# A decoder layer's gated MLP: PSUM banks from a free list, a look-ahead of one chunk, additions and low halves one product later

## The chip, the cores and the metric

The kernel runs on one core of a Trainium2 chip. Its engines run side by side, each through its own queue in order: TensorE (PE, with PEld for the loading of weights), VectorE (DVE), ScalarE (ACT), GpSimd (POOL) and SyncE (SP, which here issues every DMA). They meet at semaphores. The metric is the device time of one execution in microseconds (us); lower is better. "Lnnn" is a line of the kernel before.

## What is computed

One layer: a mixing sub-layer (pooling and dilated attention), then a channel sub-layer, a gated MLP with a causal convolution of width 3. The change touches the second:

```python
def conv_ffn(h, w_up, conv_w, conv_b, w_down):
    S = h.shape[1]
    up = h @ w_up
    gate, val = up[..., :D_FF], up[..., D_FF:]
    gp = jnp.pad(gate, ((0, 0), (CONV_WIDTH - 1, 0), (0, 0)))
    gate = gp[:, 0:S] * conv_w[0] + gp[:, 1:S + 1] * conv_w[1] + gp[:, 2:S + 2] * conv_w[2] + conv_b
    return (jax.nn.gelu(gate, approximate=True) * val) @ w_down
```

SEQ and D_MODEL are 1024, D_FF is 2816, everything is float32. Every norm has an adaLN modulation; its gate for this sub-layer, a row of 1024 numbers, is worked out from `w_ada` during the MLP.

## The kernel before

**The up product.** D_FF is cut into 22 chunks of 128 channels. Per chunk the kernel needs four blocks, gate and value for two halves of the sequence, each 128x512, and gets them by Strassen's scheme with seven products instead of eight. A product is a sum over four blocks of 128 of the contraction, and each factor is split in a high and a low part of float32 (high·high, high·low, low·high), so that a product is 12 matmuls (L1042 to L1044) into one PSUM bank of 128x512. Products are written (n, c): n from 1 to 7, c the chunk. Products 1 and 2 make the gate of the first half of the sequence, 5, 6, 3, 7 and 4 the rest.

**What each product needs.** Its stationary side is a piece of `w_up` or a sum of pieces. `prep(n, c)` (L1119) issues the DMA or has POOL add the sums t1, t2, t3, t4 (L1117), has ACT round the high half (L119) and DVE subtract the low half (L171). It runs LEAD = 6 products ahead, and finished pieces lie in a ring of seven. `raw4` holds two chunks of raw weights (`load4`, 1024 KB each).

**What follows each product.** DVE adds it from PSUM into `UU` (u), `VV` (v) and `GG`: `evac` is issued straight after the product (n = 6: L1052 and L1053; 3: L1055; 7: L1057 and L1058; 4: L1063), and `first(c)` takes products 1 and 2 (an ACT copy, then DVE at L1021). After product 4 ACT multiplies `GG` by the last tap (L1064), DVE adds the two other taps (L1146, L1148), ACT applies GELU (L1150) and DVE multiplies with the value (L1153, `gated`). Every second chunk has four more DVE subtractions and additions (L1165, `act_sum`) for the down product. Results go to DRAM (`gscr`).

**The order.** PE, ACT, DVE and POOL run exactly in the order in which the code issues (`manual_schedule`). `steps` (L1168) lists the products: chunk by chunk 5, then the 4 of the chunk before, 6, two products of look-ahead (2 and 1 of a later chunk), 3, 7. Products 1 and 2 of chunks 0 to 3 are made before the loop (AHEAD = 3). In the chunks of `SKIP` = (0, 7, 14) and in the last chunk there is no look-ahead: such a chunk has five products instead of seven. With the last product, (4, 21), `steps` has 146.

**Banks.** PSUM has eight banks, and `SLOTS` gives chunk c the pair c mod 4. Look-ahead runs three chunks ahead and so holds three of the four pairs. Within a chunk, products 2, 5 and 3 write one bank of the pair, and 1, 6, 7 and 4 the other, one after another.

**The gate row.** `gate_acc` (L1183) loads eight blocks of `w_ada` (256 KB), each into the same buffer `gm`, and DVE adds each up (L1187, L1189), one block per product; this is done twice, once from 14 products before chunk 16 on and once from 14 before chunk 19 on. `gate_sum` sums over partitions with one matmul.

**Start and end.** The operands of the Strassen products (`sums` L926, `parts` L171) are made by DVE and ACT from the normed input at the turn from the mixing sub-layer; POOL does some of it (L970 four sums of weights, L926 once, L171 once). After the 146th product the down product starts on PE at once; its pieces are prepared ahead too (`prep_down`).

Of the kernel before, what the change touches and what calls it, by code (L numbers as in the profile page):

```python
# [88 lines left out]
SKIP = (0, 7, 14)  # L89
LAST_4 = 0  # L90
ENDS = 6
S_LAG = 3
# [8 lines left out]
def block_kernel(ctx: ExitStack, tc: tile.TileContext, x, pos, cols, rows, consts, w_ada_a, w_ada_b, w_in_u,  # L101
# [744 lines left out]
    if True:  # L846
# [73 lines left out]
        def sums(cols, which):  # L920
            m11, m12, m21, m22, m1 = (x[:, :, cols] for x in (a11, a12, a21, a22, SRC["s1"]))
            for i in which:
                eng, o, a, b, op = ((nc.vector, m1, m22, m21, ALU.subtract), (nc.vector, m11, m1, m11, ALU.add),
                                    (nc.vector, m12, m11, m12, ALU.subtract),
                                    (nc.vector if cols == lo_t else nc.gpsimd, m21, m11, m22, ALU.subtract))[i]
                eng.tensor_tensor(o, a, b, op)  # L926
# [9 lines left out]
        with tc.manual_schedule(engines={ET.PE, ET.Activation, ET.DVE, ET.Pool}):  # L936
# [22 lines left out]
            for c in range(AHEAD + 1):  # L959
                if c + 2 <= AHEAD:  # L960
                    up_load(c + 2)
                if c == 2:
                    raws = [rp.tile([P, 2, 512], F32, name="raws", tag="raw") for _ in range(2)]
                    raws = [t[:, i] for t in raws for i in range(2)]
                    for i in range(4):
                        nc.sync.dma_start(raws[i], w_up[0, :, i])
                    b11, b21, b12, b22 = raws
                    t2r = cp.tile([P, 512], F32, name="t2r", tag="macc")
                    for o, a, b in ((b11, b11, b12), (t2r, b11, b22), (b12, b12, b22), (b21, b21, t2r)):
                        nc.gpsimd.tensor_tensor(o, a, b, ALU.add)  # L970
                    p0 = r2.tile([P, 4, 512], F32R, name="p0", tag="r2b")
# [44 lines left out]
            def first(c):  # L1016
                if c >= NC_FF:
                    return
                a, b = (bank(x) for x in SLOTS[c % 4])
                copy(nc.scalar, UU[:, c % 2], a)  # L1020
                nc.vector.tensor_add(GG[:, c % 2, 0:512], UU[:, c % 2], b)  # L1021
# [6 lines left out]
            def new_piece():  # L1028
# [3 lines left out]
            USES = {1: ("11", 1, 0), 2: ("12", 2, 1), 3: ("s4", 3, 1), 4: ("22", "t4", 0), 5: ("s1", "t1", 1),  # L1032
                    6: ("s2", "t2", 0), 7: ("s3", "t3", 0)}

            def product(n, c):
                a, w, b = USES[n]
                wh, wl = W.pop((w, c))
                o = bank(LAST_4 if (n, c) == (4, NC_FF - 1) else SLOTS[c % 4][b])
                for k in range(4):
                    ks = slice(k * P, (k + 1) * P)  # L1040
                    ah, al = side(a, k)
                    nc.tensor.matmul(o, wh[:, ks], ah, start=k == 0, stop=False)  # L1042
                    nc.tensor.matmul(o, wh[:, ks], al, start=False, stop=False)  # L1043
                    nc.tensor.matmul(o, wl[:, ks], ah, start=False, stop=k == 3)  # L1044
# [3 lines left out]
            def evac(n, c):  # L1048
                a, b = (bank(x) for x in SLOTS[c % 4])
                u, v = UU[:, c % 2], VV[c % 3]  # L1050
                if n == 6:
                    nc.vector.tensor_sub(u, u, a)  # L1052
                    nc.vector.tensor_add(v[:, hi], u, b)  # L1053
                elif n == 3:
                    nc.vector.tensor_add(v[:, lo], v[:, hi], b)  # L1055
                elif n == 7:
                    nc.vector.tensor_add(u, u, a)  # L1057
                    nc.vector.tensor_add(v[:, hi], v[:, hi], a)  # L1058
                elif n == 4:
                    if c == NC_FF - 1:  # L1060
                        a = bank(LAST_4)
                    g = GG[:, c % 2]
                    nc.vector.tensor_add(g[:, hi], u, a)  # L1063
                    nc.scalar.activation(cv, g, AF.Identity, bias=cl("conv_b", c), scale=cl("conv_w2", c))  # L1064
                    LATER.append((0, lambda: taps(c, g)))
                    LATER.append((1, lambda: gated(c, v)))
            v, u = VV[0], UU[:, 0]
            a, b = (bank(x) for x in SLOTS[0])
# [12 lines left out]
            parts("s4", all_t)  # L1081
            nc.vector.tensor_sub(u, u, a)
            nc.vector.tensor_sub(v[:, hi], v[:, hi], a)
            product(3, 0)
            more = r1.tile(half, F32R, name="more", tag="rb2")
# [5 lines left out]
            product(7, 0)  # L1091
            evac(3, 0)
            first(1)
            A["22"] = [(0, *(r2.tile(half, F32R, name="b22", tag=t) for t in ("r2a", "r2b")))]
            parts("22", all_t, lo_eng=nc.gpsimd)
            more = r1.tile([P, 8, 512], F32R, name="more", tag="rb0")
            ring += [(more[:, 2 * i], more[:, 2 * i + 1]) for i in range(4)] + [(p1[:, 0], p1[:, 1])]
# [6 lines left out]
    with tc.manual_schedule(engines={ET.PE, ET.Activation, ET.DVE, ET.Pool}):  # L1104
# [4 lines left out]
        def fetch(src):  # L1109
            r, w = new_raw(), new_piece()  # L1110
            nc.sync.dma_start(r, src)
            split(r, *w)
            return w
# [5 lines left out]
        def prep(n, c):  # L1119
# [10 lines left out]
            elif n in (1, 2):  # L1130
                W[n, c] = fetch(w_up[c, :, n - 1])
                return
# [9 lines left out]
            W[key, c] = new_piece()  # L1142
            split(src, *W[key, c])
# [24 lines left out]
        steps, done, FIRST = [], AHEAD, {}  # L1168
        for c in range(NC_FF):
            one = []  # L1170
# [9 lines left out]
            FIRST[len(steps) - 3 + (len(ahead) == 0)] = c + 1  # L1180
# [12 lines left out]
        def gate_sum(hf, c):  # L1193
            o = bank(SLOTS[(c + 2) % 4][1])
# [3 lines left out]
            nc.vector.tensor_tensor(row, o[0:1], row, ALU.add)  # L1198
# [5 lines left out]
            LATER.append((2, fin))  # L1204

        EXTRA, LATER = {}, []
# [5 lines left out]
        for j in range(NC_FF // 2):  # L1212
            i4 = steps.index((4, 2 * j + 1))
            for i in range(4):
                EXTRA.setdefault(i4 + S_LAG + i, []).append(lambda j=j, i=i: act_sum(2 * j + 1, i))
# [33 lines left out]
        ready = [4]  # L1249

        def prep_up(to):
            while ready[0] < min(to, len(steps)):
                prep(*steps[ready[0]])
                ready[0] += 1

        prep_up(5)
        evac(7, 0)
        prep_up(6)
        for i, (n, c) in enumerate(steps):
            if i < 4:  # L1260
                continue
            for f in EXTRA.get(i, ()):
                f()
            prep_up(i + 1 + min(LEAD, i - 2))
# [18 lines left out]
        for d, f in LATER:  # L1283
            f()
        for i in sorted(EXTRA):
            if i >= len(steps):
                for f in EXTRA[i]:
                    f()

    with tc.manual_schedule(engines={ET.PE}):  # L1290
# [12 lines left out]
        def dbank(n, t):  # L1303
            return bank(((6, 7, 2, 3), (0, 1, 4, 5))[DOWN.index(n) % 2][t])
# [125 lines left out]
```

## Time and profile before

| | |
|---|---|
| median of 3 runs | 1137.0 us (1135.84 to 1140.2) |
| the profiled execution | 1138.1 us |
| its span, first to last instruction | 1136.3 us |
| PE busy | 1056.9 us (93%) |
| DVE busy | 862.7 us (76%) |
| ACT busy | 473.7 us (42%) |
| POOL busy | 239.5 us (21%) |
| mean granted clock of TensorE | 0.981 |

Matmuls overlap in the record (one of 128x512 is shown with 0.39 us, and the next starts 0.23 us after it), so PE's busy time says less than the distance from start to start. A row of the timeline has start, duration, engine, line, operation, output and inputs, and in brackets how long the engine had stood idle and what ended the wait. A row of the windows has the stretch, its length, the busy time of PE, PEld, DVE, ACT and POOL (with the number of instructions), the granted clock, the DMA share and GB/s.

### The profile page before, as it was taken

Reading aid. Unit: us, or ns where it says so; the run is one execution under the profiler, and the core shown is the slowest. Engines: PE = TensorE matmul, PEld = TensorE weight load, DVE = VectorE, ACT = ScalarE, POOL = GpSimd, SP = SyncE. Lnnn points to the kernel's source line nnn. Section 1 sums busy time; section 2 is a strip of 40 time slices with the busy share of each in tenths; the row PEclk is TensorE's granted clock in tenths of the full one; section 3 lists DMA queues with packets and bytes.
Section 4 is the critical chain, followed back from the end, with each engine's and each line's share of the span. In section 5 each row is a group of like instructions: output and inputs, shape, how many; then the busy total and the mean of one; then the engine's idle time right before and its main releaser. Section 6 shows DMA issues by size and latency. Waiting matters only on the chain.

```text
span 1136.3 us, 15489 instructions
## 1 busy us (share of the span) xinstructions
PE 1056.9 (93%) x5174; PEld 881.7 (78%) x5174; DVE 862.7 (76%) x1881; ACT 473.7 (42%) x958; POOL 239.5 (21%) x138
## 2 busy tenths in 40 slices
PE   5899999999999998889998999969979999999996
PEld 4799997889888876667777778757757888888885
DVE  8964457864657799778787887858768898856797
ACT  6564342433544686433332333322223355544542
POOL 0000000000000004433342333323233153302460
PEclk9999999999999999899999999989989999999999
DMA  9651446262211543133424332335434589666653
GB/s 351 214 165 38 136 115 187 70 192 60 82 46 39 201 151 130 47 112 130 149 78 154 112 123 109 121 112 175 143 109 139 178 289 351 193 200 216 211 187 111
DMA packets 85147, 168.32 MB, mean 148 GB/s; under 512 B 9158, under 2 KB 25926, under 8 KB 81356
## 3 DMA queue, kind: packets, MB, share of 16 engines
q1 hardware_dynamic: 85068, 167.35, 44.4%
q8 instruction: 40, 0.66, 0.2%
q14 instruction: 39, 0.32, 0.1%
HBM read 134.47 MB, written 32.84 MB: 147 GB/s over the span
## 4 chain that ended last, share of the span: by engine, by line
PE 56%; DVE 23%; DMA 8%; issue 7%; ACT 4%; POOL 1%; SPq 0%; DVEq 0%; ACTq 0%; POOLq 0%
PE PS L1311 6%; PE PS L1313 6%; PE PS L1312 6%; PE PS L1042 6%; PE PS L1044 5%; PE PS L1043 5%; PE PS L223 5%; PE PS L225 4%; PE PS L224 4%; DMA gm<-in_w_ada_b_dram 3%; DMA mraw<-in_w_ada_b_dram 2%; DVE cv L1148 2%; PE PS L686 2%; DVE more L171 2%; PE PS L656 2%
## 5 line engine op out<-in xcount | busy, mean ns | idle before, releaser
L223 PE MATMUL PS<-wh,hh 128*128 128x384 f32 x336 | 125.6, 374 | 0.0
L225 PE MATMUL PS<-wh,hl 128*128 128x384 f32 x336 | 114.3, 340 | 0.0
L224 PE MATMUL PS<-wl,hh 128*128 128x384 f32 x336 | 114.1, 340 | 0.0
L970 POOL TENSOR_TENSOR raws<-raws 128x512 f32<-128x512 f32 x2 | 4.0, 1993 | 438.9 <-DMA raws<-in_w_up_dram 438.9
L171 DVE TENSOR_TENSOR more<-raws,more 128x512 fp32r<-128x512 f32 x79 | 68.6, 876 | 27.4 <-ACT more L119 27.4
L119 ACT ACTIVATE more<-raws 128x512 fp32r<-128x512 f32 x79 | 48.8, 622 | 68.9 <-PE PS L1043 48.8
L1117 POOL TENSOR_TENSOR raws<-rw 128x512 f32<-128x512 f32 x28 | 50.9, 1818 | 94.4 <-DVE more L171 81.8
L223 PEld LDWEIGHTS PS<-wh,hh 128*128 128x128 f32 x336 | 64.1, 191 | 7.9 <-issue 4.8
L665 ACT ACTIVATE pm<-pm,nm 128x128 f32<-128x128 f32 (+1 forms) x96 | 42.4, 443 | 65.2 <-DVE nm L663 44.0
L1064 ACT ACTIVATE cv<-GG,col 128x1024 f32<-128x1024 f32 x22 | 27.4, 1244 | 98.5 <-DVE GG L1063 98.5
L224 PEld LDWEIGHTS PS<-wl,hh 128*128 128x128 f32 x336 | 64.2, 191 | 0.6 <-issue 0.5
L225 PEld LDWEIGHTS PS<-wh,hl 128*128 128x128 f32 x336 | 64.0, 190 | 0.0
L1150 ACT ACTIVATE cv<-cv 128x1024 f32<-128x1024 f32 x22 | 23.3, 1061 | 89.3 <-DVE cv L1148 89.3
L1042 PE MATMUL PS<-a,more 128*128 128x512 f32 x144 | 56.0, 389 | 0.0
L1043 PE MATMUL PS<-a,more 128*128 128x512 f32 x144 | 56.0, 389 | 0.0
L1044 PE MATMUL PS<-a,more 128*128 128x512 f32 x144 | 56.0, 389 | 0.0
L1042 PE MATMUL PS<-b,more 128*128 128x512 f32 x84 | 35.8, 427 | 20.8 <-DVE VV L1058 18.0
L659 DVE CUSTOM_DVE_ANT_0 pm<-PS,cst 128x128 f32<-128x128 f32 (+1 forms) x96 | 30.9, 348 | 30.0 <-PE PS L656 26.2
L1311 PE MATMUL PS<-tail 128*128 128x512 f32 x128 | 49.8, 389 | 0.0
L1312 PE MATMUL PS<-tail 128*128 128x512 f32 x128 | 49.8, 389 | 0.0
L1313 PE MATMUL PS<-tail 128*128 128x512 f32 x128 | 49.8, 389 | 0.0
L1148 DVE SCALAR_TENSOR_TENSOR cv<-GG,col,cv 128x1022 f32<-128x1022 f32 x22 | 47.6, 2165 | 0.7
(381 smaller groups left out, 3157.0 us busy)
## 6 DMA issues: line engine op xcount, KB each, us to landing
rw<-in_w_up_dram SPq DMA_DIRECT2D x21, 1024.0 KB
gscr<-VV SPq DMA_DIRECT2D x66, 256.0 KB
mraw<-in_w_ada_b_dram SPq DMA_DIRECT2D x48, 256.0 KB
R<-in_w_down_dram SPq DMA_DIRECT2D x48, 256.0 KB
raw<-in_w_in_u_dram SPq DMA_DIRECT2D x24, 384.0 KB
wa<-in_w_ada_a_dram SPq DMA_DIRECT2D x8, 1024.0 KB
raws<-in_w_up_dram SPq DMA_DIRECT2D x28, 256.0 KB
R<-gscr SPq DMA_DIRECT2D x27, 256.0 KB
```

Of the source, the lines that this page charges most:

```text
L171: (lo_eng or nc.vector).tensor_tensor(wl, raw, wh.bitcast(F32), ALU.subtract)
L223: nc.tensor.matmul(o, a, wh[:, c0:c0 + 384], start=k == 0, stop=False)
L224: nc.tensor.matmul(o, a, wl[:, c0:c0 + 384], start=False, stop=False)
L225: nc.tensor.matmul(o, b, wh[:, c0:c0 + 384], start=False, stop=k == 7)
L1042: nc.tensor.matmul(o, wh[:, ks], ah, start=k == 0, stop=False)
L1043: nc.tensor.matmul(o, wh[:, ks], al, start=False, stop=False)
L1044: nc.tensor.matmul(o, wl[:, ks], ah, start=False, stop=k == 3)
L1117: nc.gpsimd.tensor_tensor(t, a, b, ALU.add)
L1148: nc.vector.scalar_tensor_tensor(cv[:, 2:], g[:, :S - 2], cl("conv_w0", c), cv[:, 2:], op0=ALU.mult, op1=ALU.add)
L1311: nc.tensor.matmul(o, gh[:, ts_], wh, start=k == 0, stop=False)
L1312: nc.tensor.matmul(o, gh[:, ts_], wl, start=False, stop=False)
L1313: nc.tensor.matmul(o, gl[:, ts_], wh, start=False, stop=k == KD - 1)
```

## The change

Five things change in the up product. (1) A bank is no longer bound to a chunk: `idle` is a list of free banks, `product` takes the one that has been free longest, and `done_with` gives a bank back when the code issues its last read. (2) `SKIP` is (0, 1, 4), so that from chunk 5 on products 1 and 2 are made one chunk ahead and not three or fewer; chunks 7 and 14 have seven products, chunks 1 and 4 five. (3) `evac` and the subtraction of a low half are issued one product later (LAG_EV, LAG_LO); the high half on ACT keeps its place. (4) What was hung behind a product by lists of delays (`LATER`, `EXTRA`) is now a list of tasks by step. (5) At the start the four sums of weights (L970), one subtraction (L926) and the low half of operand 22 (L171, 128x2048) go from POOL to DVE, and 5 and 6 of chunk 0 are ordered anew.

```diff
-SKIP = (0, 7, 14)
-LAST_4 = 0
+SKIP = (0, 1, 4)
-S_LAG = 3
+LAG_LO, LAG_EV = 1, 1
...
-                    for o, a, b in ((b11, b11, b12), (t2r, b11, b22), (b12, b12, b22), (b21, b21, t2r)):
-                        nc.gpsimd.tensor_tensor(o, a, b, ALU.add)
...
+            used = {(n, c): SLOTS[c][n - 1] for c in range(AHEAD + 1) for n in (1, 2)}
+            idle = []
+
+            def done_with(n, c):
+                idle.append(used[n, c])
+                return bank(used.pop((n, c)))
 
             def product(n, c):
-                a, w, b = USES[n]
+                a, w = USES[n]
                 wh, wl = W.pop((w, c))
-                o = bank(LAST_4 if (n, c) == (4, NC_FF - 1) else SLOTS[c % 4][b])
+                used[n, c] = idle.pop(0)
+                o = bank(used[n, c])
...
                 if n == 6:
-                    nc.vector.tensor_sub(u, u, a)
-                    nc.vector.tensor_add(v[:, hi], u, b)
+                    nc.vector.tensor_sub(u, u, done_with(6, c))
+                    nc.vector.tensor_add(v[:, hi], u, done_with(5, c))
...
             sums(hi_t, (0, 1))
+            start_sum("t1", b11, b11, b12)
             start_piece("t1", b11)
             parts("s1", hi_t)
             first(0)
-            sums(hi_t, (2, 3))
+            product(5, 0)
+            sums(hi_t, (2,))
             parts("s2", hi_t)
+            start_sum("t2", t2r, b11, b22)
             start_piece("t2", t2r)
-            product(5, 0)
+            product(6, 0)
+            first(1)
             start_piece(3, b22)
-            product(6, 0)
-            nc.vector.tensor_add(v[:, hi], u, b)
             pairs_of("s4")
             parts("s4", all_t)
...
             product(3, 0)
+            sums(hi_t, (3,))
+            start_sum("t3", b12, b12, b22)
...
-            W[key, c] = new_piece()
-            split(src, *W[key, c])
+            w = W[key, c] = new_piece()
+            copy(nc.scalar, w[0], src)
+            return lambda: lower(src, *w)
...
+        def later_evac(n, c):
+            if n in (3, 4, 6, 7):
+                at_step(now[0] + LAG_EV, lambda: (evac(n, c), finish_4(c) if n == 4 else None))
...
+            to = i + 1 + min(LEAD, i - 2)
+            prep_up(to, to - LAG_LO)
...
-            due = [f for d, f in LATER if d == 0]
-            LATER[:] = [(d - 1, f) for d, f in LATER if d]
-            for f in due:
-                f()
+            run_tasks(i)
+            while not idle:
+                run_tasks(10**6, 1)
             product(n, c)
-            evac(n, c)
-            first(FIRST.get(i, NC_FF))
+            later_evac(n, c)
...
-            return bank(((6, 7, 2, 3), (0, 1, 4, 5))[DOWN.index(n) % 2][t])
+            return bank(idle[4 * (DOWN.index(n) % 2) + t])
```

**The start on DVE, before.** From the second half of the operand sums on; `p` and `more` are pieces, `s`, `s2l`, `s4l` operands, `raws` raw weights, `GG` the first chunk's gate.

```order
L926 TENSOR_TENSOR s1t<-raw_a,raw_b 128x4x256
L926 TENSOR_TENSOR raw_a<-s1t,raw_a 128x4x256
L171 TENSOR_TENSOR p_4714<-raws,p_4714 128x512
L171 TENSOR_TENSOR s_4627<-s1t,s_4627 128x4x256
L1021 TENSOR_TENSOR GG<-UU,PS 128x512
L926 TENSOR_TENSOR raw_b<-raw_a,raw_b 128x4x256
L171 TENSOR_TENSOR s2l<-raw_a,s2h 128x2x256 x2
L171 TENSOR_TENSOR p_4714<-t2r,p_4714 128x512
L171 TENSOR_TENSOR p_4779<-raws,p_4779 128x512
L1079 TENSOR_TENSOR VV_4782<-UU,PS 128x512
L171 TENSOR_TENSOR s4l<-raw_b,s4h 128x1024 x2
```

The same place on DVE in the changed kernel (its lines are its own: L1068 is `start_sum`, L924 `sums`, L170 `split`, L1016 `first`):

```order
L924 TENSOR_TENSOR s1t<-raw_a,raw_b 128x4x256
L924 TENSOR_TENSOR raw_a<-s1t,raw_a 128x4x256
L1068 TENSOR_TENSOR raws<-raws 128x512
L170 TENSOR_TENSOR p_4710<-raws,p_4710 128x512
L170 TENSOR_TENSOR s_4627<-s1t,s_4627 128x4x256
L1016 TENSOR_TENSOR GG<-UU,PS 128x512
L924 TENSOR_TENSOR raw_b<-raw_a,raw_b 128x4x256
L170 TENSOR_TENSOR s2l<-raw_a,s2h 128x2x256 x2
L1068 TENSOR_TENSOR t2r<-raws 128x512
L170 TENSOR_TENSOR p_4710<-t2r,p_4710 128x512
L1016 TENSOR_TENSOR GG<-UU,PS 128x512
L170 TENSOR_TENSOR p_4775<-raws,p_4775 128x512
```

The sums of weights now stand between the operand sums, and the second `first` has come forward ahead of operand s4.

**A chunk of the loop on ACT, before.** From the high halves around product 4 on: `cv<-GG` is the last tap, `cv<-cv` GELU, the rest are high halves; `t2r` is the sum t2.

```order
L119 ACTIVATE p_4779<-raws 128x512
L1064 ACTIVATE cv<-GG,col 128x1024
L119 ACTIVATE more<-raws 128x512
L1150 ACTIVATE cv<-cv 128x1024
L119 ACTIVATE more<-t2r 128x512
```

The same place on ACT in the changed kernel (L118 the high half, L1158 GELU):

```order
L118 ACTIVATE more<-raws 128x512 x2
L1064 ACTIVATE cv<-GG,col 128x1024
L118 ACTIVATE p_4775<-t2r 128x512
L1158 ACTIVATE cv<-cv 128x1024
L118 ACTIVATE more<-raws 128x512 x2
```

**The same chunk on DVE, before** (the addition of product 4, a low half, the taps, the additions of product 6, a low half, `gated`):

```order
L1063 TENSOR_TENSOR GG<-UU,PS 128x512
L171 TENSOR_TENSOR more<-raws,more 128x512
L1146 SCALAR_TENSOR_TENSOR cv<-GG,col,cv 128x1023
L1148 SCALAR_TENSOR_TENSOR cv<-GG,col,cv 128x1022
L1052 TENSOR_TENSOR UU<-UU,PS 128x512
L1053 TENSOR_TENSOR VV_4784<-UU,PS 128x512
L171 TENSOR_TENSOR more<-t2r,more 128x512
L1153 SCALAR_TENSOR_TENSOR VV_4783<-cv,VV_4783 128x1024
```

And in the changed kernel (L1119 is the low half, L1154 and L1156 the taps, L1161 `gated`):

```order
L1063 TENSOR_TENSOR GG<-UU,PS 128x512
L1119 TENSOR_TENSOR more<-raws,more 128x512
L1154 SCALAR_TENSOR_TENSOR cv<-GG,col,cv 128x1023
L1156 SCALAR_TENSOR_TENSOR cv<-GG,col,cv 128x1022
L1053 TENSOR_TENSOR UU<-UU,PS 128x512
L1054 TENSOR_TENSOR VV_4778<-UU,PS 128x512
L1119 TENSOR_TENSOR p_4775<-t2r,p_4775 128x512
L1161 SCALAR_TENSOR_TENSOR VV_4780<-cv,VV_4780 128x1024
```

DVE's rows read alike, but the low half between L1063 and the taps belongs to another piece: before to the one whose high half stands behind `cv<-GG` on ACT, now to one that stands ahead of it.

More of the change, by code (lines that the diff above doesn't have):

```diff
@@ L1107, in new_raw, with fetch, lower @@
             return pool_r[(at["r"] - 1) % len(pool_r)]
[L1109 removed]
+        def fetch(src, low=True):
             r, w = new_raw(), new_piece()
             nc.sync.dma_start(r, src)
[L1112 to L1113 removed]
+            copy(nc.scalar, w[0], r)
+            if low:
+                lower(r, *w)
+            return w if low else (w, r)
+        def lower(r, wh, wl):
+            nc.vector.tensor_tensor(wl, r, wh.bitcast(F32), ALU.subtract)
         def total(n, c, a, b):
@@ L1193, in gate_sum @@
         def gate_sum(hf, c):
-            o = bank(SLOTS[(c + 2) % 4][1])
+            used["gate", c] = idle.pop(0)
+            o = bank(used["gate", c])
             nc.tensor.matmul(o, ones, gm[:, 1], start=True, stop=True)
```

105 lines of the change are left out of this document (56 added, 49 removed).

## The prediction

> **What bounds it now.** First the windows, cut where product (5, c) of some chunk starts: the start of the up product, chunks 2 to 6, 7, 8 to 12, 13 to 15, 16 to 18, 19 to 21, and the down product.
>
> ```profile
> 449.10:495.30 46.20, 35.85 (x133) 27.18 (x132) 36.91 (x40) 21.29 (x31) 24.07 (x12) 0.89 0.19 63
> 495.30:598.10 102.80, 97.89 (x421) 78.20 (x422) 83.55 (x97) 33.24 (x50) 39.00 (x23) 1.00 0.35 119
> 598.10:615.50 17.40, 13.73 (x61) 11.05 (x59) 13.96 (x18) 5.90 (x9) 5.91 (x4) 1.00 0.40 131
> 615.50:718.50 103.00, 99.15 (x420) 79.21 (x420) 83.54 (x94) 34.00 (x51) 36.55 (x21) 0.98 0.34 118
> 718.50:788.10 69.60, 58.60 (x231) 45.78 (x231) 51.50 (x67) 19.07 (x29) 20.14 (x12) 0.93 0.40 136
> 788.10:860.50 72.40, 62.57 (x257) 49.67 (x255) 53.51 (x66) 20.31 (x31) 21.08 (x12) 0.95 0.39 133
> 860.50:918.10 57.60, 55.81 (x242) 44.85 (x241) 48.24 (x60) 18.89 (x29) 19.71 (x12) 1.00 0.57 190
> 918.10:1136.30 218.20, 209.62 (x925) 173.24 (x923) 170.52 (x267) 102.12 (x194) 65.02 (x39) 0.99 0.64 215
> ```
>
> Then PE's timeline, for the price of a product and for the gaps.
>
> ```profile
> 561.55 0.47 PE L1042 MATMUL PS<-b,more 128*128 128x512 f32 x1 [1.62 <-DVE VV L1058]
> ...
> 567.12 0.39 PE L1042 MATMUL PS<-a,more 128*128 128x512 f32 x1
> 569.84 0.39 PE L1042 MATMUL PS<-a,more 128*128 128x512 f32 x1
> ...
> 615.53 0.50 PE L1042 MATMUL PS<-s,p 128*128 128x512 f32 x1 [3.70 <-DVE GG L1021]
> ...
> 616.75 0.63 PE L1043 MATMUL PS<-s,p 128*128 128x512 f32 x1
> ```
>
> 567.12 and 569.84 are the first matmuls of two products in a row: 2.72 us each, 0.227 a matmul. 146 products cost 397.1 us. The up product takes 469.0 (449.1 to 918.1), so 72 are lost: by stretch (length less 11, 35, 5, 35, 19, 21 and 20 products) 16.3, 7.6, 3.8, 7.8, 17.9, 15.3 and 3.2. The down product's 218 us are dense already. What PE waits for in the up product, by the waits (total, times, longest):
>
> ```profile
> PE PS L1042 <- DVE VV L1058: 18.0, 10, 3.7
> PE PS L1042 <- DVE GG L1021: 14.3, 5, 4.9
> PE PS L1042 <- DVE VV L1053: 8.4, 6, 3.8
> ```
>
> All three are banks that DVE has not read yet. The usual one, at 561.55, is product 4 waiting for the second addition of 7, whose bank it shares, two products after it. And behind a long gap (615.53) a matmul is shown with 0.63 us instead of 0.39: the clock is down, and the windows with such gaps have 0.93 to 0.95.
>
> **Banks and look-ahead.** I counted the list through by the new code. From chunk 6 on a bank goes back six or seven products before it is used again, so DVE may be some 15 us late (16.3 less what it is late anyhow); before it was one or two products. That ends the three waits wherever DVE is not later than this: 7.6, 3.8 (the five-product chunk 7, where DVE needs more than PE) and 7.8 go. Chunks 1 and 4, now short, stand where DVE's backlog is small; two such chunks add under 3 us each to it. Products 1 and 2 keep their cost and their two 256 KB loads each, still issued six products (16.3 us) ahead on SP (eight loads of that size in a row, with DVE's part between, take 32 us further down, 4 each).
>
> The extra wait on low halves I cost at nothing: they are issued five products ahead, and the product at 569.84, with two waits long met, starts without a gap. Were every low half only just in time, the nearest row is 561.55, a matmul that did wait: 0.08 longer than the others, 12 us in 146 products, which is the other end.
>
> **Start.** DVE and POOL work beside each other there:
>
> ```profile
> 435.57 1.22 DVE L926 TENSOR_TENSOR s1t<-raw_a,raw_b 128x1024 f32<-128x1024 f32 x1
> ...
> 440.36 2.33 DVE L171 TENSOR_TENSOR s<-s1t,s 128x1024 fp32r<-128x1024 f32 x1
> ...
> 450.12 3.38 DVE L171 TENSOR_TENSOR s<-s1t,s 128x1024 fp32r<-128x1024 f32 x1
> 453.42 0.67 DVE L1021 TENSOR_TENSOR GG<-UU,PS 128x512 f32<-128x512 f32 x1
> ```
> ```profile
> 439.35 2.25 POOL L970 TENSOR_TENSOR raws<-raws 128x512 f32<-128x512 f32 x1 [438.91 <-DMA raws<-in_w_up_dram]
> ...
> 449.75 2.67 POOL L926 TENSOR_TENSOR raw_b<-raw_a 128x1024 f32<-128x1024 f32 x1 [2.49 <-DVE raw_a L926]
> ...
> 469.19 5.01 POOL L171 TENSOR_TENSOR b<-raw_a,b 128x2048 fp32r<-128x2048 f32 x1
> ```
> ```profile
> 454.15 0.79 PE L1042 MATMUL PS<-s,p 128*128 128x512 f32 x1 [4.89 <-DVE GG L1021]
> ...
> 474.91 0.50 PE L1042 MATMUL PS<-b,more 128*128 128x512 f32 x1 [2.52 <-ACT more L119]
> ```
>
> A DVE instruction of 128x1024 takes 1.22, and 2.3 to 3.4 beside POOL. Walking the new order: DVE gains about 6.5 (1.1 and 2.2 at two of the rows, as much again on their neighbours) and spends 0.6 on the first sum; operand s is split at about 449, and product (5, 0), which now needs only ACT's copy out of its bank, starts at about 449.5 instead of 454.15, at full clock (the stretch's clock of 0.89 is some 10 us at half, 5 lost). What POOL gave away costs DVE 5.2 behind that: three sums at 0.6, L926 1.14, the 2048-wide half 2.3. So product (6, 0) waits about 1 us for the sum t2, and (7, 0) about 5 for its low halves; the wait at 474.91, behind the 5.01 on POOL, goes. I keep 7 of the 16.3 lost (0 to 21.5: all hidden, or nothing gained and DVE's 5.2 on top).
>
> The Trainium skill, "SBUF — State Buffer", section "Who interferes with whom", says that a DVE instruction with two SBUF inputs and a GpSimd one that reads SBUF exclude each other for a whole instruction. The rows agree in kind (2.33 beside 2.25); by the rule DVE would get back all of POOL's time, some 10 us instead of 6.5, and the sum would be 3 lower.
>
> **DVE as the next bound.** What DVE waits for in the up product, and how busy it is in two windows that part at 738:
>
> ```profile
> DVE more L171 <- ACT more L119: 44.1, 34, 3.9
> DVE gm L1189 <- DMA gm<-in_w_ada_b_dram: 22.4, 11, 5.8
> DVE GG L1063 <- PE PS L1044: 19.8, 16, 2.0
> DVE p L171 <- ACT p L119: 5.5, 8, 1.8
> ```
> ```profile
> 738.02:925.10 187.08, 166.61 (x683) 132.32 (x682) 143.87 (x178) 58.01 (x88) 59.84 (x34) 0.95 0.46 155
> 449.10:738.02 288.92, 263.99 (x1107) 209.41 (x1107) 233.75 (x266) 100.37 (x148) 112.10 (x61) 0.98 0.32 111
> ```
>
> It is 377.6 us busy from 449.1 to the last addition of product 4 at 925.14. Now the 44.1: one is this.
>
> ```profile
> 564.60 0.69 DVE L1063 TENSOR_TENSOR GG<-UU,PS 128x512 f32<-128x512 f32 x1 [1.39 <-PE PS L1044]
> 567.17 0.69 DVE L171 TENSOR_TENSOR more<-raws,more 128x512 fp32r<-128x512 f32 x1 [1.89 <-ACT more L119]
> ```
> ```profile
> 565.38 1.24 ACT L1064 ACTIVATE cv<-GG,col 128x1024 f32<-128x1024 f32 x1 [4.95 <-DVE GG L1063]
> 566.53 0.61 ACT L119 ACTIVATE more<-raws 128x512 fp32r<-128x512 f32 x1
> ```
>
> The low half waits for its high half, which stands on ACT behind the 1.24 of the last tap. In the new order it belongs to a high half ahead of that, so that DVE does it in those 1.24 and then waits about 0.7 for the tap itself: 22 times 0.7 is 15.4 instead of most of 44.1. The DMA wait stays, because `gm` is still one buffer: each of the eight blocks is loaded only after DVE has used the last. DVE's first and last of the eight, twice:
>
> ```profile
> 738.02 0.48 DVE L1187 TENSOR_SCALAR gm<-gm,cact 128x512 f32<-128x512 f32 x1
> ...
> 770.00 0.74 DVE L1189 SCALAR_TENSOR_TENSOR gm<-gm,cact 128x512 f32<-128x512 f32 x1
> ...
> 812.72 0.48 DVE L1187 TENSOR_SCALAR gm<-gm,cact 128x512 f32<-128x512 f32 x1
> ...
> 842.54 0.75 DVE L1189 SCALAR_TENSOR_TENSOR gm<-gm,cact 128x512 f32<-128x512 f32 x1 [1.03 <-DMA gm<-in_w_ada_b_dram]
> ...
> 925.14 0.68 DVE L1063 TENSOR_TENSOR GG<-UU,PS 128x512 f32<-128x512 f32 x1
> ```
>
> 32.0 and 29.8 us, while PE does seven products in 19: DVE falls 11 to 13 behind each time. The slack of 15 takes the first; two chunks later DVE has made up only about 3 (16.7 of work a chunk, 83.54 in five, and 0.7 of wait against PE's 19.0), and the second makes PE wait 8 to 10.
>
> **The sum.** PE's floor: 449.1 + 397.1 + 1.7 (the gate's matmuls) + 7 = 854.9. DVE's: 449.2 + 377.9 (377.6, less the 4.3 up to 453.42, done before 449.2 now, less 0.6 for one addition fewer, plus 5.2) + 22.4 + 15.4 + 3 (start) = 867.9 for its last addition. That now comes 7.7 after PE's end at 918.1 (925.8), and the down product does not wait for it; so PE could end at 860.2. DVE also waits for PE in quiet chunks, 1.6 in each of chunks 10 to 13 once its backlog is worked off (+6), and I add 2 for half-clock after PE's waits: 868. So 918.1 − 868 = 50 us fewer: 1138.1 − 50 = 1088 for the profiled execution. That lies 1.1 above the median; I forecast **1087**.
>
> **Rivals.**
> - DVE keeps its waits for ACT, because ACT's high halves also wait for PE to leave the ring. All 49.6 of them (44.1 and 5.5 on `p`) instead of 15.4 put DVE's end 34 later: PE ends at about 894 to 900, **1112 to 1118**. Against it: the high half now has a product's time more. Chance 0.13.
> - The list does nothing (banks return too late, PE stays one product behind DVE): only the start (9) and part of the short chunks (about 8) is gained: **1120**. My count of six to seven products speaks against it: 0.02.
> - Slower: DVE's in-order queue carries all of today's waits, 92 us in the four rows and those for PE among them, plus the 15.4 and the moved work: 449.2 + 377.9 + 92 + 15.4 = 934.5, less 7.7 is 926.8, 8.7 later than now: **1147**. It decides from 99 us of DVE waits on (918.1 + 7.7 − 449.2 − 377.9). The 19.8 for PE speak against it: they exist because DVE is ahead. 0.03.
> - PE at half the clock: a product then costs 5.4 instead of 2.7, and 18 of 146 products at that rate take back all 50. The stretch 495.3 to 598.1, which goes round all eight banks with gaps, has a clock of 1.00. 0.02, spread over 1100 to 1140. The Trainium skill, "TensorE: Matmul & The Clock Gate", section "A second HAM failure mode: psum-queue depth-cycling", reports such a loss from cycling through banks with short idles; that row speaks against it here.
> - Better: `gm` waits overlap and the start hides all: PE's floor less 4, **1070**. 0.08.
>
> **Numbers.** The forecast itself, 1074 to 1104, has 0.72. The range 1071 to 1110 takes in some of both neighbours. A measurement tells 0.5% (5.7 us) from no change: faster 0.95, same 0.02, slower 0.03.
>
> **What would show it.** The first up product at about 449.5; 19.0 us from (5, c) to (5, c+1) in chunks 5 to 13 without a bank wait of L1058's kind; DVE's waits for ACT at 15 to 20 us; PE's waits gathered in the chunks 17 to 19; up product over at about 868 on PE. It is wrong if PE waits for low halves at every product, if DVE is never idle from chunk 2 on, or if the down product, which DVE's backlog runs into, has gaps of more than 2 us.

## The result and the profile after

| | before | after |
|---|---|---|
| median of 4 runs each, on one chip | 1138.3 us | 1080.4 us (1079.1 to 1082.7) |
| ratio, 95% interval | | 0.9495 (0.9468 to 0.9521) |
| span of the profiled execution | 1136.3 us | 1078.3 us |
| up product on PE, from the end of the phase ahead to its last matmul | 469.0 us | 412.6 us |
| rest after it | 218.2 us | 218.3 us |

The change is worth 5.0%, and 56.4 of the 58.0 us by which the two spans differ lie in the up product. The other 1.7 lie ahead of it: the up product starts at 447.4 instead of 449.1. That is no gain to explain: in nine profiled executions of kernels that issue the same instructions up to there it started anywhere from 445.5 to 451.9. So stretches of the up product are compared below, and not spans.

The windows of the changed kernel, cut where products (5, 3), (5, 13) and (5, 19) start and where the down product starts (columns as in the windows of before):

```profile
447.40:501.28 53.88, 48.36 (x193) 37.90 (x192) 48.98 (x54) 24.43 (x34) 22.66 (x14) 0.94 0.21 69
501.28:686.24 184.96, 184.96 (x817) 153.20 (x816) 167.56 (x195) 68.60 (x98) 66.67 (x42) 1.00 0.40 140
686.24:805.12 118.88, 116.83 (x509) 94.89 (x508) 97.35 (x121) 37.40 (x55) 36.58 (x23) 1.00 0.46 151
805.12:859.97 54.85, 54.85 (x242) 45.23 (x241) 53.48 (x67) 20.81 (x33) 26.21 (x13) 1.00 0.59 203
859.97:1078.20 218.23, 209.70 (x925) 173.17 (x923) 173.82 (x269) 102.77 (x195) 65.53 (x40) 0.99 0.65 219
```

The second row is the reading that matters most: PE's busy time equals the length of the stretch, for ten chunks in a row, at full clock. 68 products take 184.96 us, 2.72 each. What a stretch loses is its length less 2.72 for each of its products (16, 68, 42 and 20 here; before, with more products in the first, 18, 68, 40 and 20):

| lost, us | start to chunk 2 | chunks 3 to 12 | chunks 13 to 18 (both gates) | chunks 19 to 21 |
|---|---|---|---|---|
| before | 18.3 | 17.3 | 33.1 | 3.3 |
| after | 10.4 | 0.1 | 4.7 | 0.5 |

What PE still waits for in the up product (total, times, longest):

```profile
PE PS L1045 <- DVE s3l L170: 2.1, 1, 2.1
PE PS L1046 <- DVE more L1119: 1.4, 3, 0.5
PE PS L1044 <- DVE VV L1060: 1.3, 1, 1.3
PE PS L1044 <- ACT p L118: 0.9, 1, 0.9
PE PS L1046 <- DVE p L170: 0.7, 1, 0.7
PE PS L1046 <- DVE p L1119: 0.6, 1, 0.6
PE PS L1044 <- ACT s3h L118: 0.5, 1, 0.5
```

Of the 40.7 us of waits for banks one is left, 1.3 us in chunk 2 (L1060). New in the loop are waits for low halves (L1046 with L1119: a product's third matmul is the first to read one). All four of them stand in the second gate. PE's timeline there:

```profile
789.00 0.50 PE L1046 MATMUL PS<-s2h,p 128*128 128x512 f32 x1 [0.63 <-DVE p L1119]
792.53 0.50 PE L1046 MATMUL PS<-a,more 128*128 128x512 f32 x1 [0.51 <-DVE more L1119]
796.06 0.50 PE L1046 MATMUL PS<-a,more 128*128 128x512 f32 x1 [0.47 <-DVE more L1119]
799.51 0.50 PE L1046 MATMUL PS<-s4h,more 128*128 128x512 f32 x1 [0.43 <-DVE more L1119]
```

And DVE's:

```profile
794.64 0.75 DVE L1197 SCALAR_TENSOR_TENSOR gm<-gm,cact 128x512 f32<-128x512 f32 x1 [1.58 <-DMA gm<-in_w_ada_b_dram]
795.31 0.69 DVE L1119 TENSOR_TENSOR more<-raws,more 128x512 fp32r<-128x512 f32 x1
```

DVE waits for a block of the gate, adds it up, then makes the low half, done at 796.00; PE's matmul that needs it starts at 796.06. PE moves in step with the loads of the gate here, one product in 3.5 us.

From such pairs one number can be read for each product: DVE's **lead**, from the end of the low half to the start of the matmul that reads it.

| lead, us, at product | (5, 13) | (2, 17), behind gate 1 | (4, 16), ahead of gate 2 | (1, 19), in gate 2 | (4, 21) |
|---|---|---|---|---|---|
| after | 15.4 | 5.6 | 11.3 | 0.06 | 9.9 |

The first gate costs PE nothing but its own matmul: it is paid out of the lead. The second finds only part of it made good, and takes 3.3 us from PE (the 4.7 of the table less 1.4, which is what ev0, below, loses there without any wait). In the chunks away from the start and the gates, "quiet" from here on (3 to 12), the lead is 7 to 15 us.

### The profile page after: what moved, and what is told of

Read it like the earlier page. It is cut to its first block, busy times and chain, and to the rows that moved or that the text cites. A ratio compares the mean times of both kernels' runs of the same rounds, so it can differ in the third digit from the quotient of the medians.

```text
span 1078.3 us, 15477 instructions
## 1 busy us (share of the span) xinstructions
PE 1038.9 (96%) x5174; PEld 876.9 (81%) x5174; DVE 860.6 (80%) x1886; ACT 474.8 (44%) x958; POOL 217.9 (20%) x132
## 4 chain that ended last, share of the span: by engine, by line
PE 73%; DVE 16%; DMA 5%; ACT 3%; issue 2%; SPq 0%; POOL 0%; DVEq 0%; ACTq 0%; POOLq 0%
PE PS L1044 9%; PE PS L1045 9%; PE PS L1046 9%; PE PS L1345 6%; PE PS L1344 6%; PE PS L1346 6%; PE PS L222 5%; PE PS L224 5%; PE PS L223 5%; PE PS L685 3%; PE PS L655 2%; DMA gm<-in_w_ada_b_dram 2%; DMA mraw<-in_w_ada_b_dram 2%; PE PS L675 1%; DVE more L1119 1%
## 5 line engine op out<-in xcount | busy, mean ns | idle before, releaser
L1123 POOL TENSOR_TENSOR raws<-rw 128x512 f32<-128x512 f32 x30 | 45.5, 1516 | 512.5 <-DVE t2r L1068 450.3
L118 ACT ACTIVATE more<-raws 128x512 fp32r<-128x512 f32 x81 | 49.6, 624 | 67.0 <-PE PS L1045 53.1
L1119 DVE TENSOR_TENSOR more<-raws,more 128x512 fp32r<-128x512 f32 x75 | 71.7, 958 | 3.1 <-ACT more L118 3.1
L1046 PE MATMUL PS<-a,more 128*128 128x512 f32 x144 | 56.3, 391 | 1.0 <-DVE more L1119 1.0
L658 DVE CUSTOM_DVE_ANT_0 pm<-PS,cst 128x128 f32<-128x128 f32 (+1 forms) x96 | 30.8, 348 | 29.7 <-PE PS L655 22.6
L1158 ACT ACTIVATE cv<-cv 128x1024 f32<-128x1024 f32 x22 | 23.4, 1062 | 57.9 <-DVE cv L1156 57.9
L1154 DVE SCALAR_TENSOR_TENSOR cv<-GG,col,cv 128x1023 f32<-128x1023 f32 x22 | 36.9, 1678 | 11.4 <-ACT cv L1064 11.4
L170 DVE TENSOR_TENSOR wl<-raw,wh 128x768 fp32r<-128x768 f32 (+1 forms) x34 | 34.8, 1033 | 12.0 <-ACT wh L118 11.8
L489 DVE SCALAR_TENSOR_TENSOR macc<-mraw,cact,macc 128x512 f32<-128x512 f32 x42 | 31.4, 748 | 15.6 <-DMA mraw<-in_w_ada_b_dram 15.4
```

What stands on the lines that cost most here:

```text
L118: nc.scalar.activation(o, i, AF.Copy)
L1119: nc.vector.tensor_tensor(wl, r, wh.bitcast(F32), ALU.subtract)
L1123: nc.gpsimd.tensor_tensor(t, a, b, ALU.add)
```

## Experiments

The losses of all kernels in the up product, and their times. Each ratio is to the kernel before, on the same chip.

| kernel | median, us | ratio, interval | to chunk 2 | 3 to 12 | 13 to 18 | 19 to 21 |
|---|---|---|---|---|---|---|
| again | 1079.9 | 0.950 (0.948 to 0.952) | 10.3 | 0.1 | 4.2 | 0.5 |
| bskip | 1136.0 | 1.001 (0.999 to 1.003) | 24.8 | 18.0 | 29.5 | 4.2 |
| nolist | 1118.9 | 0.984 (0.981 to 0.987) | 23.1 | 6.3 | 23.3 | 2.8 |
| nolist_ev0 | 1119.1 | 0.983 (0.981 to 0.986) | 22.8 | 7.2 | 22.6 | 2.8 |
| deep | 1082.9 | 0.955 (0.951 to 0.960) | 9.8 | 0.1 | 8.8 | 0.5 |
| lag00 | 1099.5 | 0.969 (0.966 to 0.973) | 14.9 | 0.1 | 9.3 | 2.2 |
| lo0 | 1094.2 | 0.965 (0.961 to 0.968) | 13.7 | 0.1 | 8.1 | 3.9 |
| ev0 | 1074.0 | 0.945 (0.943 to 0.947) | 8.6 | 0.1 | 1.4 | 0.4 |
| gate2 | 1076.2 | 0.948 (0.946 to 0.951) | 10.4 | 0.1 | 2.8 | 0.5 |
| pool4 | 1082.0 | 0.952 (0.950 to 0.954) | 11.9 | 0.1 | 4.7 | 0.5 |
| best | 1076.3 | 0.946 (0.943 to 0.949) | 9.7 | 0.1 | 1.4 | 0.4 |
| start | 1075.2 | 0.948 (0.946 to 0.949) | 7.8 | 0.1 | 1.4 | 0.4 |

**again**, the changed kernel beside three others:

> The changed kernel once more, beside the three that follow, so that differences of a few us can be read on one chip. Expected 1080 (1079 to 1083), a ratio of 0.9495 to the kernel before.

It came out so, in its time and in what each stretch loses.

### Banks and look-ahead

**bskip**, the kernel before with one line of the change:

```diff
-SKIP = (0, 7, 14)
+SKIP = (0, 1, 4)
```

> The kernel before with SKIP = (0, 1, 4) and nothing else: look-ahead of one chunk, banks still bound to chunks in pairs. My theory (product 4 still shares a bank with 7, and 3 with 5): the waits for banks stay, 1130 to 1140. Rival (a shorter look-ahead frees the banks by itself): 1100 to 1115.

No difference. The waits are those of before:

```profile
PE PS L1042 <- DVE VV L1058: 19.6, 9, 5.2
PE PS L1042 <- DVE GG L1021: 15.3, 5, 5.7
...
PE PS L1042 <- DVE VV L1053: 9.0, 5, 3.7
```

**deep**, the changed kernel with the old look-ahead:

```diff
-SKIP = (0, 1, 4)
+SKIP = (0, 7, 14)
```

> SKIP is (0, 7, 14) again, so products 1 and 2 are made three chunks ahead and hold up to six of the eight banks; the list and the lags stay. My theory (the list is worth what free banks it has): a bank is used again one or two products after it comes free, the bank waits are back in most chunks, 1105 to 1130. Rival (the list and the lags bring the gain, whatever the look-ahead): 1080 to 1086.

My expectation fell: with six banks held by the look-ahead, chunks 3 to 12 still lose nothing. Only the gates cost more, 8.8 instead of 4.2 to 4.7; the longest wait there, 1.5 us, is for a bank again. Its up product takes 416.2 us against 412.1 and 412.6; by their medians the two kernels can't be told apart (the intervals overlap).

**nolist** and **nolist_ev0**, the changed kernel with the banks of before, the second without the lag of the additions as well:

```diff
-                used[n, c] = idle.pop(0)
+                used[n, c] = 0 if (n, c) == (4, NC_FF - 1) else SLOTS[c % 4][n in (2, 3, 5)]
...
-            used["gate", c] = idle.pop(0)
+            used["gate", c] = SLOTS[(c + 2) % 4][1]
...
-            return bank(idle[4 * (DOWN.index(n) % 2) + t])
+            return bank(((6, 7, 2, 3), (0, 1, 4, 5))[DOWN.index(n) % 2][t])
```

In the start of both, products (3, 0) and (7, 0) are written over (5, 0) and (6, 0) before DVE has read these, since the new order of the start counts on free banks. So what they compute is no longer the layer. Every instruction is still there, but their first stretch is not compared.

> The changed kernel with its banks bound to chunks in pairs again (product 4 shares one with 7, 3 with 5), and nothing else undone: look-ahead of one chunk, both lags and the new start stay. Lags at 0 left chunks 3 to 12 without a loss, and a look-ahead of three chunks did too, so by what is left (the list is what takes the bank waits away) these chunks lose 15 us again as in the kernel before, and the gates more than 4: 1100 to 1125. Rival (list, lags and look-ahead can each stand in for the others): 1080 to 1088.

> As nolist, with the additions from PSUM straight after their product, as the kernel before has them, so that a fixed bank is not kept a product longer by the lag. If only the lag with fixed banks were at fault: 1075 to 1085. If the fixed banks are: 1095 to 1120, with waits of PE for the second addition of product 7 in most chunks.

The times are as expected and the lag of the additions makes no difference there. But the place was not: the ten quiet chunks lose 6.3, not 15, and 23.3 go in the gates; and in nolist_ev0 PE waits for the second addition of 7 in four chunks, not in most. Of the 40 us that nolist's up product takes longer than that of again (452.4 against 412.1), 13 lie in the stretch that is not compared; what the fixed banks can be shown to cost is the other 27. The longest waits of nolist for banks:

```profile
PE PS L1044 <- DVE GG L1016: 11.3, 3, 6.4
PE PS L1044 <- DVE VV L1054: 10.4, 4, 5.6
PE PS L1044 <- DVE VV L1060: 7.3, 3, 4.1
```

Few waits, but long ones: with a bank to a pair of products PE meets DVE's lateness at once, where the list lets it pass until it reaches the low halves. So the list is what the change can't do without, while in the quiet chunks the rest of it (the lags, the new order of the tasks: which of them is not shown) does much of the work too, 17.3 us lost before against 6.3 here. No run has the list alone, with the old look-ahead and without the lags.

### The lags

**lo0** and **lag00**:

```diff
-LAG_LO, LAG_EV = 1, 1
+LAG_LO, LAG_EV = 0, 1
```

(lag00 has 0, 0.)

> The low half is subtracted in the same step as its high half is rounded, as in the kernel before; all else stays. My theory (this lag takes DVE's waits for ACT away): DVE's waits for ACT in the up product go from about 20 us to 40 to 50, it cannot make its lead good between the two gates, and PE waits at the second gate and behind it, 8 to 14 us more: 1088 to 1094. Rival (bank list and look-ahead bring the whole gain, DVE's waits for ACT cost nothing once banks are free): 1079 to 1082.

> Both lags at 0: the bank list, the look-ahead of one chunk and the new start alone. My theory: 1091 to 1097, as with the low halves alone and 2 to 3 us for the additions. Rival (list and look-ahead bring the whole gain): 1079 to 1082. Second rival (the lags bring most of it): over 1110.

By the medians lo0 is 14 us slower than again (on another chip), 0.2 above the range that I expected; in the traces the up product and the rest together take 12.6 us more. lag00 is 2.5 us slower than its range; between the two the intervals overlap. DVE's waits for ACT in lo0's up product:

```profile
DVE p L1119 <- ACT p L118: 26.5, 14, 1.9
DVE more L1119 <- ACT more L118: 25.6, 29, 2.4
```

52.1 us instead of 7.1 (in exchange for the 11.4 for the tap), and yet chunks 3 to 12 lose nothing. The loss comes at the start, in the gates and behind them, where DVE can't make good what it is late; and the down product starts late on some pieces (220.7 us instead of 218.3, in lag00 226.5). It is not low halves that stop PE in lo0's gates: these stay at least 4.2 us ahead there, since each stands a product earlier in DVE's queue. PE's two long waits, in chunk 18, are for banks that DVE's additions have not read:

```profile
PE PS L1044 <- DVE UU L1053: 7.2, 2, 4.0
```

So a late DVE can stop PE at the banks as well as at the low halves, and the lead of the low halves alone does not tell.

**ev0**:

```diff
-LAG_LO, LAG_EV = 1, 1
+LAG_LO, LAG_EV = 1, 0
```

> The additions from PSUM are issued straight after their product again, the rest stays. My theory (what counts is how early DVE finishes a low half before PE's third matmul asks for it; the bank list removed the bank waits by itself): DVE must wait for the product in front of it more often and can be at most about 13 us early instead of 15, so the second gate takes some 2 to 3 us more from PE: 1082 to 1084, and no bank waits of over 1 us behind chunk 2. Rival (the later additions are what made the bank waits go): bank waits come back in every chunk, 1095 or more. Second rival (the place of the additions does not matter): 1080.

None of the three held: it is 6 us faster than the changed kernel, and the intervals do not touch (0.9431 to 0.9474 against 0.9475 to 0.9522 for again); its up product takes 407.5 us in the profile, against 412.1 and 412.6. The lag of the additions costs time. What the setting changes is narrower than its name. In the code both values issue the additions in the step behind their product, after that step's low half: 1 puts them behind the other tasks which the step already holds (the taps, `gated`), 0 ahead of these. (The kernel before has them ahead of the low half as well.) So for the additions "one product later" is a place behind these tasks, and ev0 tests that place. DVE's waits in the up product, first in the changed kernel:

```profile
DVE gm L1197 <- DMA gm<-in_w_ada_b_dram: 18.5, 12, 4.9
DVE cv L1154 <- ACT cv L1064: 11.4, 18, 1.4
DVE more L1119 <- ACT more L118: 7.1, 6, 1.6
DVE GG L1063 <- PE PS L1046: 5.5, 6, 1.5
DVE UU L1059 <- PE PS L1046: 1.4, 3, 0.6
DVE VV L1161 <- ACT cv L1158: 1.3, 1, 1.3
...
```

And in ev0:

```profile
DVE gm L1197 <- DMA gm<-in_w_ada_b_dram: 17.5, 11, 5.5
DVE more L1119 <- ACT more L118: 8.0, 6, 1.7
DVE VV L1161 <- ACT cv L1158: 7.7, 13, 0.7
DVE UU L1053 <- PE PS L1046: 7.6, 6, 1.4
DVE GG L1063 <- PE PS L1046: 4.6, 3, 1.5
...
DVE cv L1154 <- ACT cv L1064: 0.8, 1, 0.8
```

Without the lag the two additions of product 6 stand ahead of the taps, so that DVE works while ACT does the last tap (11.4 becomes 0.8), and it waits more for GELU (1.3 becomes 7.7). On balance DVE waits less for ACT and more for PE, that is, for want of work. Its smallest lead in the second gate is 0.7 us instead of 0.06, PE's waits there are gone, and so is the one in chunk 2: there the additions of product 7 now stand ahead of `gated` and its wait, and end 1.4 us after (6, 2) starts instead of 4.1.

### The gates

**gate2**, the eight blocks at every second product:

```diff
-                EXTRA.setdefault(i - 14 + kb, []).append(
+                EXTRA.setdefault(i - 17 + 2 * kb, []).append(
```

> The eight blocks of the gate row stand at every second product instead of at every product. My theory (in the second gate DVE waits for the loads into the one buffer until it has no lead left, and PE then waits for low halves four times): DVE's waits for these loads fall from 18.5 us to under 5, its smallest lead behind chunk 3 stays over 4 us, PE's waits at the second gate (3.4 us) go: 1076 to 1077.5. Rival (DVE's lead is lost to its own work for the gates, not to the loads): PE still waits, 1079 to 1081.

The waits for the loads fall from 18.5 us to 7.4 (L1197 and L1195), not to under 5; the smallest lead behind chunk 3 rises to 4.0, and no product of the loop waits for a low half any more. PE's two longest waits behind the start are now:

```profile
PE PS L1044 <- DVE VV L1060: 1.3, 1, 1.3
PE PS L1204 <- DVE gm L1197: 1.2, 1, 1.2
```

The gate's own matmul (L1204) now waits 1.2, since its last block is added up only three products ahead. The stretch loses 2.8 instead of 4.2 to 4.7. The trace shows the mechanism; the time alone would not, since its interval overlaps that of again.

### The start

**pool4**, the four sums of weights on POOL again:

```diff
+                    for o, a, b in ((b11, b11, b12), (t2r, b11, b22), (b12, b12, b22), (b21, b21, t2r)):
+                        nc.gpsimd.tensor_tensor(o, a, b, ALU.add)
...
                 TR[n, 0] = o
-                nc.vector.tensor_tensor(o, a, b, ALU.add)
```

> The four sums of weights at the start are on POOL again, at their old place; the subtraction and the low half of operand 22 stay on DVE, and the new order stays. My theory (POOL's work beside DVE lengthens DVE's instructions from 1.2 to 2.3 to 3.4 us): the first up product starts 2 to 5 us later, at 449 to 452 instead of 447.4, DVE does three sums of 0.6 us less behind it: 1081 to 1085 in all. Rival (the new order of products and operands brought the early start, not POOL's absence): 1079 to 1080.5.

The mechanism is as expected. The same sum on DVE, in the changed kernel and then in pool4, and what POOL does beside it there:

```profile
440.99 1.22 DVE L924 TENSOR_TENSOR s1t<-raw_a,raw_b 128x1024 f32<-128x1024 f32 x1
```
```profile
444.51 2.32 DVE L924 TENSOR_TENSOR s1t<-raw_a,raw_b 128x1024 f32<-128x1024 f32 x1
```
```profile
444.00 1.75 POOL L968 TENSOR_TENSOR raws<-raws,t2r 128x512 f32<-128x512 f32 x1
```

Little of it reaches PE. The first product starts 0.9 us behind the phase ahead of it (in the changed kernel it follows without a gap), and the first nine products lose 11.0 instead of 8.6. Together that is 3.3 us, of which it gets 1.8 back by not waiting in chunk 2. By the medians the two kernels differ by 2 us and can't be told apart. **best** and **start** try the order on DVE, both on top of ev0:

```diff
             product(5, 0)
-            sums(hi_t, (2,))
-            parts("s2", hi_t)
             start_sum("t2", t2r, b11, b22)
-            start_piece("t2", t2r)
+            w2 = W["t2", 0] = new_piece()
+            copy(nc.scalar, w2[0], t2r)
+            sums(hi_t, (2,))
+            nc.vector.tensor_tensor(w2[1], t2r, w2[0].bitcast(F32), ALU.subtract)
+            parts("s2", hi_t)
...
         prep_up(5, 5)
+        ring += [(p1[:, 0], p1[:, 1])]
+        prep_up(6, 6)
         parts("22", all_t)
         more = r1.tile([P, 8, 512], F32R, name="more", tag="rb0")
-        ring += [(more[:, 2 * i], more[:, 2 * i + 1]) for i in range(4)] + [(p1[:, 0], p1[:, 1])]
-        prep_up(6, 6)
+        ring += [(more[:, 2 * i], more[:, 2 * i + 1]) for i in range(4)]
```

That is start. In best the sum t4 has moved up too, to behind the low half of t2, the low half of 22 stands behind `evac(3, 0)`, and the gate has its blocks at every second product, the first half two chunks earlier.

> Additions straight after the product, the gate's blocks at every second product and its first half two chunks earlier, and a start in which DVE makes the sums t2 and t4 ahead of the operand sum and the low half of operand 22 behind that of s3. By the leads and waits of the other runs: no waits at the gates (0 to 1 us more than with the additions alone), and of the 8.6 us lost at the start 3 to 6 are won (no wait for the sum t2, less for the low half of s3, no half clock behind them): 1067 to 1072. If DVE's work at the start is the bound whatever its order: 1073 to 1075.

> Additions straight after the product as in ev0, the gates as in the changed kernel, and another order at the start: the sum t2 ahead of the operand sum, the low half of operand 22 behind the first low half of chunk 1. Unlike best, t4 stays where it was, so that POOL does not begin its sums of chunk 1 between the operands. If POOL beside DVE is what spoiled best (its s2l and s3l took 2.4 and 4.4 us instead of 1.3 and 2.4): the start loses 4 to 7 us instead of 8.6, and the time is 1069 to 1072. If DVE's own work is the bound at the start: 8 to 9 lost, 1073 to 1075.

Both are within the noise of ev0, and neither reached the times hoped for. In best the start lost more, not less (9.7 instead of 8.6). DVE's and POOL's timelines show where DVE lost time; that this alone made the difference is not shown, since other pieces moved too. DVE's:

```profile
460.98 4.43 DVE L170 TENSOR_TENSOR s3l<-raw_b,s3h 128x1024 fp32r<-128x1024 f32 x2 [0.26 <-ACT s3h L118]
```

And POOL's at the same time:

```profile
460.80 1.30 POOL L1126 TENSOR_TENSOR raws<-rw 128x512 f32<-128x512 f32 x1 [7.22 <-DVE more L170]
462.06 2.26 POOL L1126 TENSOR_TENSOR raws<-t2r,rw 128x512 f32<-128x512 f32 x1
```

The earlier t4 set POOL free to begin with chunk 1 in the middle of DVE's operands. In start, with POOL idle there, the same two instructions on DVE take 2.36:

```profile
458.23 2.36 DVE L170 TENSOR_TENSOR s3l<-raw_b,s3h 128x1024 fp32r<-128x1024 f32 x2 [0.25 <-ACT s3h L118]
```

Alone, DVE's two take 2.36 and POOL's two some 2.6 (1.3 each, as the first of them here), 4.96 together. Side by side all four take 4.61, from 460.80 to 465.41, so nearly as long as one after the other, and both engines lose: DVE 2.07 and POOL's second addition about 1. The Trainium skill, "SBUF — State Buffer", section "Who interferes with whom", has a DVE instruction with two SBUF inputs and a POOL one that reads SBUF shut each other out for a whole instruction; the 4.61 against 4.96 agrees with it.

start itself loses 7.8 against ev0's 8.6, between its two forecasts, and its time is 0.2 above that of the rival (DVE's own work is the bound). Up to (7, 0) the trace speaks for the rival: DVE works from 444.9 to 463.1 with no break over 0.3. There PE gains, since (6, 0) to (7, 0) lose 4.6 us instead of 7.9. But behind it (6, 1) and (4, 0) lose 2.9 that they did not lose in ev0, and PE's longest wait there, 1.4, is for ACT, as are DVE's at that point. So DVE's work is not the whole bound.

## Why the prediction was right, and where it was off

I forecast 1087 and a gain of 50 us; it was 1080.4 and 58.0 in the profile. Step by step:

- **Banks.** 7.6, 3.8 and 7.8 us were to go, and they did but for 1.8 in chunk 2: chunks 3 to 12 lose 0.1. The reason given was partly too narrow. I put the list and the short look-ahead together; deep shows that the list (with the lags) does it with the long look-ahead too, and bskip that the look-ahead alone does nothing.
- **The wait for low halves** at nothing: right in every quiet chunk, where the lead is 7 to 15 us. But I expected a late DVE to stop PE at a bank, some 15 us late. In the changed kernel it is the low halves that stop it first, four times in the second gate; the term had left the gates out. (In lo0 and deep the banks stop PE there again.)
- **The start.** 7 of 16.3 us were to stay lost; the start up to chunk 2 loses 8.6. (6, 0) waits 1.6 and (7, 0) 2.6 where I had about 1 and about 5, and behind both the matmuls come at 0.43 us instead of 0.23, half clock, which I had counted only elsewhere. The half clock behind (6, 0) is not what was lost: again runs that place at full speed, (7, 0) then waits 4.3 instead of 2.6, and the start loses the same 8.6.
- **DVE's waits.** For ACT 15.4 forecast, 20.5 measured (11.4, 7.1, 1.3 and 0.7); for the gate's loads 22.4 and 18.5; for PE 6 and 6.9; its work 377.9 and 376.1. DVE's last addition of product 4 was to end at 867.9 + 6 = 873.9 and ends at 871.2. This part of the sum holds within 3 us, in part because misses of up to 5 us go both ways.
- **The step that failed** is the next one: "That now comes 7.7 after PE's end", taken over from before, and with it the choice of DVE's queue as what sets PE's end. In the changed kernel DVE's last addition ends 11.3 after PE's last matmul (859.97; the row stands below), and in ev0 still 11.0, so it is not the lag of the additions. 7.7 was only where the old waits happened to leave the two, not a limit: the low half for PE's last product was ready 9.9 us before it was read. What the end goes by is the other floor, PE's own: 854.9, less 1.7 (its start at 447.4), plus 1.6 at the start, 1.8 in chunk 2 and 3.3 in the second gate, is 859.9; it was 860.0. DVE holds PE up in these places alone and not all along its queue. That the forecast came within 7 us owes something to luck: the two floors, 854.9 and 868, lie only 13 us apart.

```profile
870.55 0.68 DVE L1063 TENSOR_TENSOR GG<-UU,PS 128x512 f32<-128x512 f32 x1
```

- **The gates.** I had DVE fall 11 to 13 behind in each, make up about 3, and PE wait 8 to 10 in the second. The lead fell by 9.8, came back by 5.7, and PE lost 3.3. The place was right (chunk 18), each size was too pessimistic. gate2 confirms the cause: fewer waits for the loads, no waits for low halves.

What was to be seen in the profile: the first up product at 449.5 (447.4, and 449.7 in again); 19.0 us from (5, c) to (5, c+1) in chunks 5 to 13 (152.3 us for eight of them); waits for ACT of 15 to 20 (20.5); PE's waits in chunks 17 to 19 (789 to 800); no gap over 2 us in the down product (the trace shows no wait of PE in it).

The rivals: "DVE keeps its waits for ACT" is what lo0 makes, and its mechanism is real, but its price was far too high: 1112 to 1118 forecast, 1094.2 measured. 47 of some 51 us of such waits fall where the low half is still ready 10 us ahead or more, and cost nothing. "The list does nothing" was priced at 1120; nolist, which takes the list away, has 1118.9, though by longer waits in the gates rather than by the same ones, and with 13 us lost in a start that can't be compared. "Slower" needed over 99 us of DVE waits; the changed kernel has 46. "Better" is half right: ev0 takes the waits out of the gates, but the start still loses 8.6. PE at half the clock did not come: the 185 us that go round the banks show a clock of 1.00. They have no idles, though, and the row that spoke against this rival has four waits of 1.2 to 1.6 us in 103 us. The Trainium skill, "TensorE: Matmul & The Clock Gate", section "A second HAM failure mode: psum-queue depth-cycling", reports such a loss from frequent short idles between groups of matmuls; no run here decides whether it holds.

The best version measured is the changed kernel with its additions ahead of the other tasks of their step (ev0, 1074.0 us), though best and start can't be told from it. What it still loses in the up product is 8.6 us at the start and about 1.8 for the gate's own matmuls.

## What to carry to other kernels

When an engine in order feeds another, follow one number through the program: how long before its use each piece is ready, and each buffer free. Waits of the feeding engine cost nothing while that lead is large; they count where a burst of other work has eaten it, and it must be made good before the next burst. Give buffers and banks out from a list where a late reader would otherwise stop the writer at once. And when a lag moves work on an in-order queue, look at what it takes away from a wait that the same work used to fill: here moving low halves won 12 to 14 us, and putting the additions behind the taps cost 5 to 6.

## What the runs showed of the hardware

- POOL's additions of 128x512 and DVE's subtractions of 128x1024 beside them lengthen each other: on DVE two took 4.43 us instead of 2.36, on POOL one of two took 2.26 instead of 1.3, and all four nearly as long as one after the other (4.61 against 4.96).
- The half clock behind short waits is not the same in each execution. In the changed kernel waits of 0.94 and 0.66 us were followed by 3 us at half clock (0.43 us a matmul instead of 0.23), in a second execution of it (again) the same place ran at full speed behind 0.92 and 0.66, and in start waits of 0.8 to 1.7 us brought none.
